# The feed-forward input projection of a two-layer trunk: seven half-size products replaced by eight plain ones with 512-column matmuls

## The chip, the cores and the metric

One core of a Trainium2 chip runs the whole program. The time is device microseconds of one execution. The kernel before took 2470.91 us, the median of 3 runs (2469.47 to 2471.38). The profiled execution is another one, of 2470.22 us, and its trace spans 2468.4 us of it; the other 1.8 us lie around the trace.

## The reference, cut to what matters

Two layers run over 512 tokens of width 1024. Each layer has a feed-forward block, a mixer of three attention kinds, a second feed-forward block and a gated per-layer input (called ple). Only the first product of a feed-forward block is changed:

```python
def swiglu(h, w_in, w_out):
    gate, up = jnp.split(h @ w_in, 2, axis=-1)
    return (jax.nn.silu(gate) * up) @ w_out

h = layer_norm(DEEPNORM_ALPHA * h + 0.5 * swiglu(h, ffa_w_in[i], ffa_w_out[i]), ln_g[i, 0], ln_b[i, 0])
```

`w_in` is 1024 x 5632 (gate and up, 2816 columns each) and `w_out` 2816 x 1024. There are four feed-forward blocks in a run: a and b in each of two layers.

## The kernel before, in words

**Three products for one.** Every projection is made in a reduced format, so each operand is held as a high part and a low remainder, and a product is the sum high x high, high x low, low x high: three matmuls into one PSUM bank (`mm3`, lines 401 to 405). The weights are split while the kernel runs. `Weights` (lines 48 to 116) loads a block of 128 x 1024 numbers with DMAs on SP's queue into one of 3 `wraw` tiles, ScalarE copies it to `whi` (line 72), and VectorE or GpSimd subtracts to get `wlo` (line 74). There are 4 pairs of `whi` and `wlo`, and `next()` prepares blocks up to 3 ahead of the one in use.

**Transposed activations.** `xT` holds the block's input, features on partitions, tokens along the free axis, as tiles `xh` and `xl`. `build_xT(t)` (lines 257 to 264) makes it for 128 tokens at a time: TensorE transposes `h[t]` into two banks of pool psA (`pa`, line 262), ScalarE copies the high part (line 254), VectorE subtracts the low (line 255). It is called for t = 0 to 3 at the end of the stage ahead, behind that stage's layer norm (lines 302 to 316) or ple update.

**The input projection before** (`ffn`, lines 420 to 535). The 2816 gate and 2816 up columns make 22 tiles of 128 + 128. Tiles 0 and 1 are plain (`part`): 8 slices of the inner dimension, three matmuls each, for gate and up, first over token columns 0 to 255 of both tiles, then over 256 to 511, so that work is there before the last tokens are. Their results lie in pools psB and psC (`pb`, `pc`). That is 2 x 2 x 2 x 8 x 3 = 192 matmuls of 256 columns.

The other 20 tiles use a Strassen-type scheme of one level (`product`, line 489). A tile's 1024 x 256 weights are cut in quarters, the 1024 x 512 activations too, and 7 products of sums and differences take the place of 8. Each product has 4 slices x 3 matmuls of 256 columns (lines 499 to 501), 84 matmuls a tile, into a gate bank of psI (`pi`) and an up bank of psA (`pa`). The price lies on the other engines. `add_sums` (lines 78 to 107) makes four sums of the weights per tile on VectorE (line 96, tiles `sa`, `sb`, `su`) and splits 7 quarters of 512 columns (lines 97 and 99). Lines 450 to 476 make sums of the activations, once per block. ScalarE takes partial results out of the banks (lines 503, 505, 507) and `close_tile` adds them up on VectorE around the Silu (lines 514 to 519).

**Behind it.** The output projection (lines 539 to 590) splits the result `g` (lines 546 and 547, tiles `gs` and `old`) and runs 512-column matmuls through `mm3` against blocks of `w_out`, 24 matmuls per block. It uses two halves of the output columns, `ps0` and `ps1`, four banks each. `ple_prepare` (lines 409 to 417), for block b only, takes two banks of psI in turn.

**What sets the order.** The order on each engine is fixed when the program is made. A planner with a model of the instructions' times places them by the order of the source and by what is ready; banks and buffers of one pool are handed out in the source's order. Each engine then runs its list strictly in turn.

Of the kernel before, what the change touches and what calls it, by code (L numbers as in the profile page):

```python
# [17 lines left out]
P = 128  # L18
S = 512
# [6 lines left out]
NC = 2  # L26
XA, XB, XV = 2, 2, ()
# [20 lines left out]
class Weights:  # L48
# [28 lines left out]

    def add_sums(self, fs, sums, first=False):

        nc = self.nc  # L80
        rest = ("s1", "s4", "s2", "a22", "s3")
        if first:
            todo = [(0, "a11"), (0, "a12"), (1, "a11"), (1, "a12")] + [(f, n) for f in range(2) for n in rest]
        else:
            todo = [(f, n) for f in range(2) for n in ("a22", "a11", "a12", "s1", "s2", "s4", "s3")]
        quarters = [None, None]

        def one(f, name, hi, lo):
            if quarters[f] is None:
                r0, r1 = self.load(fs[f][0], sums("raw")), self.load(fs[f][1], sums("raw"))  # L90
                quarters[f] = {"a11": r0[:, 0:512], "a21": r0[:, 512:1024], "a12": r1[:, 0:512], "a22": r1[:, 512:1024]}
            q = quarters[f]
            if "s1" not in q and (name == "s1" or not first):
                for s, x, y, op in (("s1", "a21", "a22", ALU.add), ("s3", "a11", "a21", ALU.subtract), ("s2", "s1", "a11", ALU.subtract), ("s4", "a12", "s2", ALU.subtract)):
                    q[s] = sums(s)
                    nc.vector.tensor_tensor(out=q[s], in0=q[x], in1=q[y], op=op)  # L96
            nc.scalar.copy(hi, q[name])  # L97
            e = nc.vector if name in ("s1", "s2", "s3") else nc.gpsimd
            e.tensor_tensor(out=lo, in0=q[name], in1=hi.bitcast(F32), op=ALU.subtract)  # L99

        for i in range(7):
            def make(i=i):
                hi, lo = self.pair()
                for j in range(2):
                    one(*todo[2 * i + j], hi[:, j * 512:(j + 1) * 512], lo[:, j * 512:(j + 1) * 512])
                return hi, lo
            self.blocks.append(make)
# [12 lines left out]
def trunk(  # L120
# [207 lines left out]
    def plan_ffn(l, w_in, w_out):  # L328
        def tile_in(f):
            return [[(lambda r, j=j: r.rearrange("p (j k c) -> p j k c", k=4, j=2)[:, j],  # L330
                      rows(w_in, l, kh * 4, 4, j * D_FF + f * P, j * D_FF + (f + 1) * P)) for j in range(2)] for kh in range(2)]

        def sums(name):
            if ln_s["new"]:
                ln_s["new"] = False
                ln_s["n"] = 0
                u = unit("su").rearrange("p a b -> p (a b)")
                ln_s["r"] = 0
                ur = unit("wr").rearrange("p a b -> p (a b)")
                ln_s["w"] = [None, None, None, ur[:, 0:1024], ur[:, 1024:]]  # L340
                ln_s["s"] = [lnp.tile([P, 1024], F32, tag="lng", name=nm("sa")), lnp.tile([P, 1024], F32, tag="lnb", name=nm("sb")), u[:, 0:1024], u[:, 1024:]]
            if name == "raw":
                ln_s["r"] += 1
                return ln_s["w"][(ln_s["r"] - 1) % 5]
            i = ln_s["n"] = ln_s["n"] + 1
            i = (i - 1) % 8
            return ln_s["s"][i // 2][:, (i % 2) * 512:(i % 2 + 1) * 512]

        for f in range(NC):
            for k, parts in enumerate(tile_in(f)):  # L350
                W.add(1024, parts, V if not W.blocks or (W.n == 0 and len(W.blocks) in XV) else None)
# [68 lines left out]
    def ffn(l, ln_i):  # L420
        ln_s["new"] = True
        GA = []

        def part(ps, us, c0, c1):
            for j in range(2):
                for k in range(KD):
                    hi, lo = (u.rearrange("p (j k c) -> p j k c", k=4, j=2)[:, j, k % 4, :] for u in us[k // 4])
                    mm3(ps[j][:, c0:c1], hi, lo, xT["hi"][:, k, c0:c1], xT["lo"][:, k, c0:c1], k == 0, k == KD - 1)

        def g_(f):  # L430
            if f % 4 == 0:
                GA.append(unit("g"))
            return GA[f // 4][:, f % 4, :]

        def evac(f, ps):
            s = slab("s")
            act(s, ps[0], AF.Silu)
            V.tensor_tensor(out=g_(f), in0=s, in1=ps[1], op=ALU.mult)

        us = [(W.next(), W.next()) for _ in range(2)]  # L440
        pss = [banks(), banks(True)]
        for f in range(2):
            part(pss[f], us[f], 0, 256)


        XH, XL = xT["hi"], xT["lo"]
        full = [unit("xf"), unit("xf")]

        B = {}
        for i, j in ((1, 1), (2, 1), (1, 2), (2, 2)):  # L450
            ks, cs = slice((i - 1) * 4, i * 4), slice((j - 1) * 256, j * 256)
            b = full[j - 1].rearrange("p a b -> p (a b)")[:, (i - 1) * 1024:i * 1024].rearrange("p (k c) -> p k c", k=4)
            (G if j == 1 else V).tensor_tensor(out=b, in0=XH[:, ks, cs].bitcast(F32), in1=XL[:, ks, cs].bitcast(F32), op=ALU.add)
            B[i, j] = b
        R = {"b11": (XH[:, 0:4, 0:256], XL[:, 0:4, 0:256]), "b21": (XH[:, 4:8, 0:256], XL[:, 4:8, 0:256]), "b22": (XH[:, 4:8, 256:512], XL[:, 4:8, 256:512])}
        todo = []
        for name, x, y in (("t1", B[1, 2], B[1, 1]), ("t3", B[2, 2], B[1, 2]), ("t2", B[2, 2], "t1"), ("t4", B[2, 1], "t2")):
            if name == "t3":
                hl = [XH[:, 0:4, 256:512], XL[:, 0:4, 256:512]]
            else:  # L460
                hl = unit(name, F32R).rearrange("p a b -> p (a b)").rearrange("p (w k c) -> p w k c", w=2, k=4)
                hl = [hl[:, 0], hl[:, 1]]
            d = {"t1": B[1, 1], "t3": B[1, 2], "t2": B[2, 2], "t4": B[2, 1]}[name]
            y = B[y] if isinstance(y, str) else y
            V.tensor_tensor(out=d, in0=x, in1=y, op=ALU.subtract)
            B[name] = d
            todo.append((name, hl, d))
# [6 lines left out]
        for x in todo:  # L474
            if x[0] != "t3":
                split_t(*x)
# [797 lines left out]
```

## Time and profile before

| What | Value |
| --- | --- |
| Median of 3 runs | 2470.91 us |
| Profiled execution | 2470.22 us |
| Its span in the trace | 2468.4 us |
| TensorE, share of the span busy | 93% |
| VectorE | 68% |
| GpSimd | 49% |
| ScalarE | 41% |
| DMA, main queue, share of 16 engines | 27.2% |
| Mean granted TensorE clock | 0.97 of 2.4 GHz |

PE is TensorE, DVE is VectorE, ACT is ScalarE, POOL is GpSimd. A matmul's duration in the trace runs from its start to the end of its last result, and the next starts before that; what a matmul costs in a stream is the distance from one start to the next. "Idle before" is the time in which the engine stood still, with what ended it. PEclk is the granted clock, 1.00 for 2.4 GHz and 0.50 for 1.2 GHz.

### The profile page before, as it was taken

The numbers are of one execution on the slowest core, as the hardware profiler recorded it, in microseconds if no ns is written. First come the engines' busy times: TensorE is split into PE (matmuls) and PEld (weight loads), VectorE is DVE, ScalarE is ACT, GpSimd is POOL, SyncE is SP. The second block draws the span as 40 slices with busy tenths as digits, with TensorE's granted clock in tenths as the row PEclk, the third lists the DMA queues.
The fourth block names the chain that finished last, engine by engine and source line by source line (L and its number), as shares of the span: only waits on it lengthen the run. The fifth ranks groups of instructions, "written<-read, shape, count | busy, mean of one in ns | idle before, by whom it ended". The sixth has DMA issues, their size and how long they took to land. (4 is left out here: it accounts for less than half of the span.)

```text
span 2468.4 us, 39369 instructions
## 1 busy us (share of the span) xinstructions
PE 2290.9 (93%) x15554; PEld 2000.7 (81%) x15554; DVE 1685.1 (68%) x2449; ACT 1022.8 (41%) x1929; POOL 1216.6 (49%) x785
## 2 busy tenths in 40 slices
PE   7999999998898899999989999999979997999998
PEld 7899888765777899988788998887657777999877
DVE  8899706559565899842589995075694668998334
ACT  4454513652452444532244544146424424445222
POOL 5555643434345655554365555424343466555542
PEclk9999999998999899999999999999999998999999
DMA  4333333211012233332323333332110122333322
GB/s 134 102 89 96 112 93 84 70 42 56 24 48 69 73 89 96 99 115 71 100 73 91 94 110 99 93 88 61 35 56 27 44 69 76 95 91 103 115 85 69
DMA packets 271272, 199.81 MB, mean 81 GB/s; under 512 B 12688, under 2 KB 236016, under 8 KB 271088
## 3 DMA queue, kind: packets, MB, share of 16 engines
q1 hardware_dynamic: 271088, 197.30, 27.2%
q8 instruction: 122, 2.00, 0.3%
q14 instruction: 62, 0.51, 0.1%
HBM read 195.17 MB, written 2.10 MB: 80 GB/s over the span
## 5 line engine op out<-in xcount | busy, mean ns | idle before, releaser
L74 POOL TENSOR_TENSOR wlo<-wraw,whi 128x1024 fp32r<-128x1024 f32 (+3 forms) x209 | 443.1, 2134 | 413.8 <-ACT whi L72 373.8
L72 ACT CAST whi<-wraw 128x1024 fp32r<-128x1024 f32 (+3 forms) x194 | 200.5, 1035 | 394.4 <-PE pi L405 156.7
L99 POOL TENSOR_TENSOR wlo<-wraw,whi 128x512 fp32r<-128x512 f32 x144 | 230.1, 1614 | 168.0 <-ACT whi L97 109.2
L499 PE MATMUL pa<-t,whi 128*128 128x256 f32 x640 | 191.3, 299 | 51.6 <-DVE g L518 27.9
L99 POOL TENSOR_TENSOR wlo<-wr,whi 128x512 fp32r<-128x512 f32 x96 | 153.9, 1616 | 132.7 <-ACT whi L97 127.9
L501 PE MATMUL pa<-t,wlo 128*128 128x256 f32 x640 | 177.8, 287 | 11.1 <-DVE wlo L99 11.1
L499 PE MATMUL pi<-xh,whi 128*128 128x256 f32 x640 | 185.5, 290 | 1.4 <-ACT whi L97 1.4
L501 PE MATMUL pa<-xh,wlo 128*128 128x256 f32 x640 | 182.1, 285 | 3.3 <-POOL wlo L99 3.3
L501 PE MATMUL pi<-xh,wlo 128*128 128x256 f32 x640 | 183.1, 286 | 0.0
L500 PE MATMUL pi<-xl,whi 128*128 128x256 f32 x640 | 183.0, 286 | 0.0
L500 PE MATMUL pa<-t,whi 128*128 128x256 f32 x640 | 182.9, 286 | 0.0
L499 PE MATMUL pa<-xh,whi 128*128 128x256 f32 x640 | 181.6, 284 | 0.0
L500 PE MATMUL pa<-xl,whi 128*128 128x256 f32 x640 | 181.6, 284 | 0.0
L499 PEld LDWEIGHTS pa<-t,whi 128*128 128x128 f32 x640 | 124.1, 194 | 67.2 <-DVE g L518 26.2
L187 ACT ACTIVATE s<-s 128x512 f32<-128x512 f32 x80 | 50.6, 632 | 258.2 <-DVE s L514 258.0
L97 ACT CAST whi<-su 128x512 fp32r<-128x512 f32 x160 | 91.7, 619 | 136.4 <-PE pi L500 118.9
L519 DVE TENSOR_TENSOR g<-g,s 128x512 f32<-128x512 f32 x80 | 140.2, 1752 | 1.1
L99 DVE TENSOR_TENSOR wlo<-su,whi 128x512 fp32r<-128x512 f32 x120 | 127.9, 1089 | 5.8 <-ACT whi L97 5.8
L501 PEld LDWEIGHTS pa<-t,wlo 128*128 128x128 f32 x640 | 121.9, 194 | 11.9 <-DVE wlo L99 11.9
L499 PEld LDWEIGHTS pi<-xh,whi 128*128 128x128 f32 x640 | 125.1, 195 | 3.8 <-ACT whi L97 1.9
L501 PEld LDWEIGHTS pa<-xh,wlo 128*128 128x128 f32 x640 | 123.5, 193 | 3.9 <-POOL wlo L99 3.9
L501 PEld LDWEIGHTS pi<-xh,wlo 128*128 128x128 f32 x640 | 124.9, 195 | 0.5 <-POOL wlo L99 0.4
(492 smaller groups left out, 7319.1 us busy)
## 6 DMA issues: line engine op xcount, KB each, us to landing
wraw<-in_ffa_w_in_dram SPq DMA_DIRECT2D x112, 256.0 KB, 3.8
wraw<-in_ffb_w_in_dram SPq DMA_DIRECT2D x112, 256.0 KB, 3.5
wraw<-in_ffa_w_out_dram SPq DMA_DIRECT2D x44, 512.0 KB, 3.8
wraw<-in_ffb_w_out_dram SPq DMA_DIRECT2D x44, 512.0 KB, 3.8
wraw<-in_mix_w_in_dram SPq DMA_DIRECT2D x40, 512.0 KB, 3.9
wr<-in_ffa_w_in_dram SPq DMA_DIRECT2D x64, 256.0 KB, 3.0
wr<-in_ffb_w_in_dram SPq DMA_DIRECT2D x64, 256.0 KB, 3.0
wraw<-in_mix_w_o_dram SPq DMA_DIRECT2D x16, 512.0 KB, 3.8
```

The lines of the kernel that those rows point to most:

```text
L72: self.nc.scalar.copy(hi[:, :width], raw[:, :width])
L74: (eng or self.nc.gpsimd).tensor_tensor(out=lo[:, c], in0=raw[:, c], in1=hi[:, c].bitcast(F32), op=ALU.subtract)
L97: nc.scalar.copy(hi, q[name])
L99: e.tensor_tensor(out=lo, in0=q[name], in1=hi.bitcast(F32), op=ALU.subtract)
L187: i = A.activation(*a, **k)
L499: T.matmul(dst, ah, bh, start=start and k == 0, stop=False, skip_group_check=True)
L500: T.matmul(dst, ah, bl, start=False, stop=False, skip_group_check=True)
L501: T.matmul(dst, al, bh, start=False, stop=k == 3, skip_group_check=True)
L519: V.tensor_tensor(out=g, in0=g, in1=s, op=ALU.mult)
```

## The change

All 22 tiles of the input projection are plain. They are taken two at a time: 11 steps, each with the gate of both tiles and then the up of both. A step has four weight blocks of 128 x 1024: (gate, inner slices 0 to 3), (gate, 4 to 7), (up, 0 to 3), (up, 4 to 7), each with 256 columns for the two tiles. A tile has 2 x 8 x 3 = 48 matmuls of 512 columns; in the first step alone the tokens are still taken in two halves of 256 columns, gate first in both halves, then up. Steps with an even number use two banks of psI (gate) and two of psA (up), the others psB and psC. Of a step's four low parts the first is subtracted on VectorE, the second and fourth on GpSimd, and the third on VectorE in every second step. `add_sums`, the sums of activations, `product` and `close_tile` are gone. `xh` and `xl` are two halves of one tile; `ps0` and `ps1` of the output projection take other banks.

```diff
-    def add_sums(self, fs, sums, first=False):
...
     def new_xT():
-        xT["hi"] = xp.tile([P, KD, S], F32R, tag="xh", name=nm("xh"))
-        xT["lo"] = xp.tile([P, KD, S], F32R, tag="xl", name=nm("xl"))
+        xT["x"] = xp.tile([P, 2, KD, S], F32R, tag="x", name=nm("x"))
+        xT["hi"], xT["lo"] = xT["x"][:, 0], xT["x"][:, 1]
...
     def plan_ffn(l, w_in, w_out):
...
-        for f in range(NC, NF, 2):
-            W.add_sums([tile_in(f), tile_in(f + 1)], sums, f == NC)
+        for f in range(0, NF, 2):
+            for i in range(2):
+                for j in range(2):
+                    W.add(1024, [(lambda r: r.rearrange("p (k c) -> p k c", k=4), rows(w_in, l, j * 4, 4, i * D_FF + f * P, i * D_FF + (f + 2) * P))],
+                          G if j or (i and f % 4) else V)
...
     def ffn(l, ln_i):
...
+        def part(ps, us, f, c0, c1):
+            for k in range(KD):
+                hi, lo = (u[:, (k % 4) * 256 + f * P:(k % 4) * 256 + (f + 1) * P] for u in us[k // 4])
+                mm3(ps[:, c0:c1], hi, lo, XH[:, k, c0:c1], XL[:, k, c0:c1], k == 0, k == KD - 1)
+
+        for i in range(NF // 2):
+            b = banks4() if i % 2 == 0 else banks() + banks(True)
+            sl = [slab("s"), slab("s")]
             for j in range(2):
+                us = (W.next(), W.next())
+                for c0, c1 in ((0, 256), (256, 512)) if i == 0 else ((0, 512),):
+                    for f in range(2):
+                        part(b[2 * j + f], us, f, c0, c1)
+                if j == 0:
+                    for f in range(2):
+                        act(sl[f], b[f], AF.Silu)
+                else:
+                    if i % 2 == 0:
+                        GA.append(unit("g"))
+                    for f in range(2):
+                        V.tensor_tensor(out=GA[i // 2][:, (i % 2) * 2 + f, :], in0=sl[f], in1=b[2 + f], op=ALU.mult)
...
-        ps0 = banks() + [ibank(), ibank()]
+        ps0 = banks() + banks(True)
...
-        ps1 = banks(True) + banks()
+        ps1 = [ibank(), ibank()] + banks()
```

## Rows read from the trace of the kernel before

**Rows 1.** The page's first line

```profile
span 2468.4 us, 39369 instructions
```

**Rows 2.** Windows: stretch, us, busy (x count) of PE, PEld, DVE, ACT, POOL; PEclk; DMA

```profile
41.40:283.40 242.00, 221.99 (x1722) 214.73 (x1721) 214.02 (x239) 116.24 (x232) 136.77 (x84) 0.98 0.32 91
...
814.20:1057.90 243.70, 222.00 (x1723) 215.17 (x1722) 217.42 (x242) 115.33 (x228) 139.72 (x85) 0.96 0.31 91
...
1269.40:1507.90 238.50, 220.61 (x1722) 212.76 (x1722) 211.93 (x237) 113.47 (x226) 135.61 (x84) 0.99 0.32 94
...
2041.00:2284.80 243.80, 220.79 (x1722) 214.07 (x1721) 217.45 (x241) 113.58 (x227) 140.25 (x84) 0.96 0.31 91
```

**Rows 3.** Lines by form: product matmuls (whole run), and output-projection ones in 41.4 to 283.4

```profile
L499 PE MATMUL pa<-t,whi 128*128 128x256 f32 x640 | 191.3, 299 | 51.6 <-DVE g L518 27.9 <-ACT s L503 21.5
...
L403 PE MATMUL pb<-whi,gs 128*128 128x512 f32 x10 | 3.6, 392 | 0.0
```

**Rows 4.** Timeline of PE: start, duration; six 256-column matmuls on, in the product stage

```profile
2205.71 0.28 PE L501 MATMUL pa<-t,wlo 128*128 128x256 f32 x1
...
2206.43 0.28 PE L501 MATMUL pa<-t,wlo 128*128 128x256 f32 x1
```

**Rows 5.** Waits of PE in the whole run: total us, times, longest us

```profile
PE pa L499 <- DVE g L518: 27.9, 37, 5.5
PE pa L499 <- ACT s L503: 21.5, 22, 2.0
```

**Rows 6.** Timeline of PE: six 512-column matmuls on, in the output projection

```profile
310.57 0.39 PE L403 MATMUL pi<-whi,old 128*128 128x512 f32 x1
...
311.93 0.39 PE L403 MATMUL pi<-whi,old 128*128 128x512 f32 x1
```

**Rows 7.** Timeline of PE: five 512-column matmuls on, in the mixer's projection

```profile
480.28 0.40 PE L403 MATMUL pi<-xh,whi 128*128 128x512 f32 x1
...
481.44 0.39 PE L405 MATMUL pi<-xh,wlo 128*128 128x512 f32 x1
```

**Rows 8.** Splitting and closing work: lines by form; then line source (min/median/max ns)

```profile
L72 ACT CAST whi<-wraw 128x1024 fp32r<-128x1024 f32 x180 | 188.7, 1050 | 381.3 <-PE pi L405 156.7 <-PE pb L405 123.5 <-PE pi L404 23.1
L74 POOL TENSOR_TENSOR wlo<-wraw,whi 128x1024 fp32r<-128x1024 f32 x139 | 353.7, 2552 | 318.1 <-ACT whi L72 285.2 <-issue 26.0 <-DVE gs L547 6.8
...
L74 DVE TENSOR_TENSOR wlo<-wraw,whi x33: 630/684/1226, 9.0 to 1688.2; 128x512 fp32r<-128x512 f32 x32, 128x1024 fp32r<-128x1024 f32 x1
...
L438 DVE TENSOR_TENSOR g<-s,pb x4: 672/674/689, 40.6 to 2041.5; 128x512 f32<-128x512 f32 x4
```

**Rows 9.** Windows: 60 us of the output projection

```profile
300.00:360.00 60.00, 60.00 (x267) 49.67 (x266) 5.36 (x8) 11.58 (x11) 28.36 (x12) 1.00 0.34 105
```

**Rows 10.** Windows: the four starts, from the first plain matmul to the first product

```profile
9.50:41.40 31.90, 29.31 (x209) 28.85 (x210) 30.38 (x37) 13.24 (x18) 19.61 (x9) 0.95 0.58 155
...
785.00:814.20 29.20, 27.78 (x212) 27.02 (x213) 22.41 (x26) 9.03 (x15) 19.20 (x10) 0.90 0.24 69
...
1240.30:1269.40 29.10, 26.52 (x208) 26.31 (x209) 28.23 (x21) 11.34 (x18) 19.50 (x8) 0.94 0.20 56
...
2009.00:2041.00 32.00, 28.64 (x212) 27.98 (x213) 28.15 (x26) 10.12 (x16) 20.29 (x11) 0.84 0.17 51
```

**Rows 11.** Timeline of PE: the last transposes of tokens at each start

```profile
22.58 0.96 PE L262 MATMUL pa<-ident,h 128*128 128x128 f32 x4 [1.89 <-DVE xl L255]
...
802.82 0.60 PE L262 MATMUL pa<-ident,h 128*128 128x128 f32 x4
...
1252.82 0.38 PE L262 MATMUL pa<-ident,h 128*128 128x128 f32 x2
...
2029.55 0.60 PE L262 MATMUL pa<-ident,h 128*128 128x128 f32 x4
```

**Rows 12.** One long wait in the product stage (timeline of PE), and the clock behind it (windows)

```profile
831.12 0.58 PE L501 MATMUL pa<-t,wlo 128*128 128x256 f32 x1 [5.06 <-DVE wlo L99]
...
831.00:836.00 5.00, 4.32 (x18) 4.03 (x19) 5.00 (x8) 1.78 (x4) 1.53 (x1) 0.50 0.18 52
```

More of the change, by code (lines that the diff above doesn't have):

```diff
@@ L76, in add @@
         self.blocks.append(make)
-    def add_sums(self, fs, sums, first=False):
[L80 to L107, printed above, removed]
     def fill(self, n):
@@ L328, in plan_ffn @@
     def plan_ffn(l, w_in, w_out):
[L329 to L351, printed above, removed]
-        for f in range(NC, NF, 2):
-            W.add_sums([tile_in(f), tile_in(f + 1)], sums, f == NC)
+        for f in range(0, NF, 2):
[3 more added lines that the diff above has]
+                          G if j or (i and f % 4) else V)
         for n in range(2):
@@ L435, in evac @@
[L435 to L467, printed above, removed]
@@ L469, in split_t @@
-        def split_t(name, hl, d):
-            A.copy(hl[0], d)
-            G.tensor_tensor(out=hl[1], in0=d, in1=hl[0].bitcast(F32), op=ALU.subtract)
-            R[name] = hl
-        for x in todo:
-            if x[0] != "t3":
-                split_t(*x)
-        for f in range(2):
-            part(pss[f], us[f], 256, 512)
-            evac(f, pss[f])
-        for f in range(2, NC):
-            u = (W.next(), W.next())
-            ps = banks(f % 2 == 1)
-            part(ps, u, 0, 512)
-            evac(f, ps)
@@ L485, in ffn @@
-        if NC > 2:
-            split_t(*todo[1])
-        blk = {"n": 0}
-        def product(ps, name, start):
-            up = name in ("t4", "b11", "t2", "t3")
-            dst = ps["up" if up else "gate"][:, 0:256] if name in ("t4", "b21") else ps["up" if up else "gate"][:, 256:512]
-            j = blk["n"] % 2
-            blk["n"] += 1
-            if j == 0:
-                blk["w"] = W.next()
-            hi, lo = (w_[:, j * 512:(j + 1) * 512] for w_ in blk["w"])
-            for k in range(4):
-                ah, al, bh, bl = hi[:, k * P:(k + 1) * P], lo[:, k * P:(k + 1) * P], R[name][0][:, k, :], R[name][1][:, k, :]
-                T.matmul(dst, ah, bh, start=start and k == 0, stop=False, skip_group_check=True)
-                T.matmul(dst, ah, bl, start=False, stop=False, skip_group_check=True)
-                T.matmul(dst, al, bh, start=False, stop=k == 3, skip_group_check=True)
-            if name == "b11":
-                A.copy(ps["s"][:, 0:256], dst)
-            elif name == "t1":
-                A.copy(ps["s5"], dst)
-            elif name == "t2":
-                A.copy(ps["s"][:, 256:512], dst)
@@ L509, in open_tile @@
-        def open_tile():
-            return {"gate": ibank(), "up": bank(), "s": slab("s"), "s5": slab("s5", 256)}
-        def close_tile(f, ps):
-            g, gate, up, s, s5 = g_(f), ps["gate"], ps["up"], ps["s"], ps["s5"]
-            V.tensor_tensor(out=s, in0=s, in1=gate, op=ALU.add)
-            act(s, s, AF.Silu)
-            V.tensor_tensor(out=g[:, 256:], in0=s5, in1=up[:, 256:], op=ALU.add)
-            V.tensor_copy(s5, up[:, 256:])
-            V.tensor_tensor(out=g[:, 0:256], in0=s5, in1=up[:, 0:256], op=ALU.add)
-            V.tensor_tensor(out=g, in0=g, in1=s, op=ALU.mult)
@@ L521, in ffn @@
[L521 to L535 removed]
+        XH, XL = xT["hi"], xT["lo"]
@@ L556, in split_unit @@
             if not spare:
-                old = [xp.tile([P, KD, S], F32R, tag=tag, name=nm("old")) for tag in ("xh", "xl")]
-                spare.extend(o[:, 4 * i:4 * i + 4, :] for o in old for i in range(2))
+                old = xp.tile([P, 2, KD, S], F32R, tag="x", name=nm("old"))
+                spare.extend(old[:, j, 4 * i:4 * i + 4, :] for j in range(2) for i in range(2))
             return spare[len(HL) - 5]
```

27 lines of the change are left out of this document (1 added, 26 removed).

## The prediction
> **What bounds the kernel now.** The page says that TensorE is busy for 93% of a span of 2468.4 us [rows 1], so I looked first at whether its busy time is full of work. The windows over the four product stages (20 tiles each, from the first product to the last) take 242.0, 243.7, 238.5 and 243.8 us, 968.0 together, at clocks of 0.96 to 0.99, and VectorE is busy for 212 to 217 us of each [rows 2]. The lines by form give the number of products: one group of 640 is 80 tiles x 2 products x 4 slices, so 7 products with three matmuls a slice are 6720 in all, 1680 a stage. The other 42 of the 1722 are taken as output-projection matmuls, 512 columns wide, that the planner drew forward [rows 2, 3].
>
> Then the timeline, for what a matmul costs. Six 256-column matmuls take 2206.43 - 2205.71 = 0.72 us, 0.120 each [rows 4]. Six 512-column ones take 311.93 - 310.57 = 1.36 us, 0.2267 each [rows 6]. So a stage holds 1680 x 0.120 = 201.6 us of products and 42 x 0.2267 = 9.5 of others, and the four hold 4 x 211.1 = 844.5 us. The remaining 123.5 us are waits, and slow clock behind waits. The waits view names their causes: an up bank that VectorE has not yet closed (27.9 us, L518), a bank that ScalarE has not yet emptied (21.5 us, L503) [rows 5]. One wait of 5.06 us for a weight remainder on VectorE is followed by a window at clock 0.50, 1.2 GHz [rows 12]. The reader should see two engines at their limit: TensorE has the work, and VectorE, nine tenths busy with making seven products out of eight, makes it stop about 1.5 us a tile (123.5 / 80).
>
> **The change part by part.**
>
> Matmuls. 80 tiles x 84 x 0.120 = 806.4 us go. 80 x 48 = 3840 matmuls of 512 columns come, at 0.2267: 870.5 us. That is 64.1 us **more**, all on TensorE and so on the path. The first two tiles of each block keep 192 matmuls of 256 columns. The 0.2267 is from the output projection; in the mixer's projection, which has the operands of the new code, five steps took 481.44 - 480.28 = 1.16 us, 0.232 each [rows 7]. I take 0.2267, since in that stretch VectorE is nearly idle [rows 9], which is nearer to the new stage than the crowded mixer. The other end is 3840 x 0.0053 = 20 us dearer; below 0.2267 nothing shows a gain.
>
> The Trainium skill, in TensorE: Matmul & The Clock Gate, section on the 56 ns gap, puts the distance of two matmuls at the columns over 2.4 GHz plus 2.5 ns. By this a product tile would cost 84 x 109.2 ns = 9.17 us and a plain one 48 x 215.8 ns = 10.36, 95 us more in 80 tiles and not 64, which speaks against the change. The trace doesn't agree: both widths stand 13.3 ns above their columns' time, and halving the number of matmuls saves that per matmul.
>
> Waits. With the sums, five partial drains and the closing additions gone, the 123.5 us lose their causes. Is something late next? A step of two tiles lasts 96 x 0.2267 = 21.8 us. In it ScalarE has four casts of 1.05 us and two Silus like the one that the old plain tiles had; GpSimd has two or three remainders of 2.55, at most 7.7 us; VectorE one or two of 1.23 to 2.55 (its single row of this width is the 1.226, GpSimd's is the upper bound) and two multiplications of 0.67, at most 6.4 us [rows 8]. Each is under a third of the step. A block serves 24 matmuls, 5.4 us, exactly as in the output projection, where one cast and one GpSimd remainder per block let TensorE run 60.00 of 60 us [rows 9]. The buffers hold two sets of two blocks. A set is 48 matmuls, 10.9 us; its first pair of buffers comes free after 36 of them, at 8.2 us, its second at the end; the refill takes 1.05 + 2.55 = 3.6 us and isn't wanted before 21.8. What queues behind a waiting cast on ScalarE is the Silu, whose bank is wanted two steps later. So the steady waits cost nothing; I leave 4 us (1 per block) for the first sets. Bounds: 0, and the third rival.
>
> The start of each block. Before, the first halves of two tiles were 96 matmuls, 11.5 us, that needed no late tokens. Now the up banks come from psA, which `build_xT` holds until the last transposes are emptied, so only the gate's 48 matmuls, 5.8 us, can run ahead, and 144 x 0.120 = 17.3 us must follow the last tokens. Those were transposed at 22.58, 802.82, 1252.82 and 2029.55 [rows 11]. Adding 2 us for transposing and emptying (an estimate; the four transposes alone show 0.4 to 1.0) and 17.3, the first pair would end at 41.9, 822.1, 1272.1 and 2048.9, against 41.4, 814.2, 1269.4 and 2041.0 now [rows 10]: 19.0 us later in sum if the tokens come no earlier. They should: their transposes stood in TensorE's list behind plain matmuls, and GpSimd and VectorE had the activation sums between the norm's steps. I take half of it off, and less for the fresh remainder on VectorE: +8 us. Bounds: the four starts last 122.2 us for 4 x 192 x 0.120 = 92.2 us of work, so at best 30 us less; at worst the 19, and the clock. The clocks of 0.84 to 0.95 mean that the worst start loses 32.0 x 0.16 = 5.1 us to it and all four 11.3 [rows 10]; all as bad as the worst would be 9 us more, +28.
>
> Smaller edits together. `ple_prepare` now waits for the first banks of `ps1`, since those are psI's: its eight transposes and four drains move into the tail of two blocks, beside the norm. I price it at 2 us, 0 to 8 (four drains of up to 1 us each, twice). The merged `x` tile, the loads of 256 instead of 128 columns (same bytes) and the free buffers of the sums cost nothing: DMA engines are a third busy in these windows [rows 2].
>
> Sum against the profiled execution: 2470.2 + 64.1 - 123.5 + 4 + 8 + 2 = 2424.8, about **2425 us**. The median of the runs is 0.7 us above the profiled execution, so it stands for both.
>
> **The rivals.**
>
> Late starts. The cover of 5.8 us is too short in every block, TensorE idles until the tokens are there, and it resumes at half clock. The +28 takes the place of the +8: 2445 us. For it: the clock of the start at 2009, 0.84 [rows 10], and the 0.50 behind a 5 us wait [rows 12]. Against it: the tokens' chain loses work. The Trainium skill, same page, section on why this matters, warns that a gap without matmuls puts the array back to half clock; rows 12 agree.
>
> Dearer wide matmuls. The new stage runs at the mixer's 0.232 [rows 7]: 20 us more, 2445. For it: same operands. Against: the mixer's engines are crowded.
>
> Late weights, **slower**. A set's two blocks are now released together instead of one by one. If the list of ScalarE or GpSimd lets the second block's conversion begin only as its set begins, its 3.6 us [rows 8] stand against 12 matmuls of the first block, 2.7 us, and each of 80 sets waits 0.9 us: 72 us more, 2497. It decides from 45 / 80 = 0.57 us a set. For it: before, the very same pair of engines held TensorE up at 1.5 us a tile. Against it: 10 us of slack per refill, and a third of the load.
>
> The page's fixed cost, with 95 for 64: 2456. The rows of both widths speak against it.
>
> **How the numbers follow.** Forecast 0.73, late starts 0.12, dearer matmuls 0.07, late weights 0.06, the page's cost 0.02. The forecast's own low end is starts that gain 8 us and no leftovers: 2403, say 2404. Upwards the late starts and dearer matmuls reach 2445, and with part of both 2452; what is left out above, late weights and both together, is about 0.1. A measurement of this kernel can tell about 0.2%, 5 us, from no change. Late starts and dearer matmuls together would end within it; I give that 0.04 out of their 0.19. Slower is the late weights, 0.06. Faster takes the rest, 0.90.
>
> **What would show it.** Right: from the second step on, matmuls 0.227 us apart without idle rows, some 217.6 us for 20 tiles; VectorE under a third busy there; no wait on L99, L503 or L518 and none in their place; clock 1.00. The starts show one gap between gate's first and second halves. Wrong: distances of 0.232 or more; idle of PE on `wlo` or `whi` at every set; a gap of over 5 us at each start with a clock of 0.5 after it; transposes of `ple_prepare` in front of the last norm.

## The result, and the profile after

The changed kernel took 2406.55 us, the median of 4 runs (2402.44 to 2414.78), against 2471.14 before on the same chip: a ratio of 0.9737, 95% interval 0.9705 to 0.9769. The forecast of 2425 lies 18 us above it, and 2406.55 lies in the range of 2404 to 2452, near its low end. The profiled execution is the longest of the four, 2414.78 us; stages are compared on its trace and, where it matters, on that of a second profiled execution of the same kernel (2406.48 us, run e1).

The page's first lines of the changed kernel:

```profile
span 2413.1 us, 30778 instructions
...
PE 2322.0 (96%) x12674; PEld 1903.3 (79%) x12674; DVE 910.9 (38%) x1612; ACT 799.3 (33%) x1273; POOL 860.0 (36%) x534
```

VectorE has fallen from 68% to 38% of the span, and TensorE has risen from 93% to 96%. The windows from the second step to the end of the eleventh (20 tiles) answer to [rows 2], with the same columns:

```profile
38.03:255.66 217.63, 217.63 (x962) 180.25 (x961) 35.38 (x38) 60.23 (x68) 63.60 (x27) 1.00 0.32 97
...
811.11:1028.70 217.59, 217.59 (x962) 180.25 (x961) 35.33 (x38) 58.73 (x66) 63.56 (x27) 1.00 0.32 99
...
1246.30:1464.00 217.70, 217.70 (x963) 180.32 (x962) 35.40 (x38) 60.24 (x69) 63.63 (x27) 1.00 0.31 97
...
2006.20:2223.80 217.60, 217.60 (x962) 180.19 (x961) 35.34 (x38) 58.73 (x66) 63.57 (x27) 1.00 0.32 99
```

TensorE's busy time equals the window in all four, at clock 1.00; ScalarE and GpSimd are busy for under 30% of it and VectorE for 16%. The timeline of PE in such a stretch, six matmuls apart:

```profile
899.77 0.39 PE L352 MATMUL pb<-x,whi 128*128 128x512 f32 x1
...
901.13 0.39 PE L352 MATMUL pb<-x,whi 128*128 128x512 f32 x1
```

901.13 - 899.77 = 1.36 us, 0.2267 each, as in [rows 6]. Among the waits of PE of the whole run, no wait of the input projection for weights or banks is left; its first matmuls wait 2.7 us in sum for tokens (L222). Of the four longest groups, L223 and L272 are the tokens and the norm, the other two stand in the mixer:

```profile
PE pa L230 <- DVE x L223: 18.5, 10, 4.0
PE pa L841 <- DVE K L842: 13.7, 4, 5.0
PE pi L351 <- DVE y L699: 11.7, 2, 5.8
PE pa L230 <- DVE ln_mv L272: 6.4, 2, 3.2
```

The four starts, answering to [rows 10], and then (timeline of PE) the last transposes of tokens, answering to [rows 11]:

```profile
9.78:38.03 28.25, 27.67 (x208) 27.38 (x209) 10.96 (x28) 13.05 (x17) 7.36 (x4) 1.00 0.54 180
...
781.08:811.11 30.03, 28.42 (x212) 27.83 (x213) 11.10 (x20) 9.72 (x13) 8.48 (x6) 0.89 0.38 124
...
1216.70:1246.30 29.60, 27.64 (x209) 27.34 (x209) 7.97 (x9) 7.17 (x10) 4.14 (x3) 0.87 0.22 67
...
1978.50:2006.20 27.70, 27.22 (x213) 26.77 (x213) 10.67 (x18) 9.76 (x13) 8.46 (x6) 0.93 0.40 128
```

```profile
20.57 0.60 PE L230 MATMUL pa<-ident,h 128*128 128x128 f32 x4
...
793.55 0.60 PE L230 MATMUL pa<-ident,h 128*128 128x128 f32 x4
...
1228.63 0.60 PE L230 MATMUL pa<-ident,h 128*128 128x128 f32 x4
...
1988.54 0.60 PE L230 MATMUL pa<-ident,h 128*128 128x128 f32 x4
```

The starts are shorter by some 6.5 us in sum. The last tokens come 10.8, 12.5, 11.9 and 10.0 us behind the first matmul, where they came 13.1, 17.8, 12.5 and 20.6 us behind it [rows 10, 11].

One stage grew. Windows over the two mixers, first of the kernel before, then of the changed one:

```profile
395.10:785.00 389.90, 358.00 (x2638) 279.15 (x2637) 251.91 (x544) 177.60 (x383) 159.13 (x146) 0.96 0.20 56
1619.50:2009.00 389.50, 359.59 (x2639) 281.04 (x2637) 246.62 (x545) 178.00 (x382) 157.29 (x146) 0.96 0.20 57
```

```profile
376.04:781.08 405.04, 372.15 (x2640) 290.62 (x2638) 254.91 (x545) 177.64 (x381) 154.77 (x144) 0.93 0.18 51
1584.40:1978.50 394.10, 360.47 (x2640) 280.67 (x2638) 252.87 (x547) 176.96 (x381) 154.02 (x144) 0.96 0.18 53
```

The first mixer has the same matmuls, 14 us more of busy time (372.15 against 358.00) and 33 us idle as against 32. The changed kernel's windows show where:

```profile
685.00:695.00 10.00, 8.99 (x53) 5.86 (x52) 4.31 (x11) 1.40 (x4) 1.26 (x2) 0.52 0.23 75
695.00:705.00 10.00, 10.00 (x81) 8.99 (x81) 5.09 (x19) 4.61 (x10) 5.31 (x4) 0.50 0.00 0
705.00:716.00 11.00, 11.00 (x68) 8.65 (x67) 3.80 (x11) 4.97 (x12) 3.66 (x3) 0.50 0.01 1
```

For 30.7 us, with TensorE busy nearly throughout, the granted clock is 0.50 (1.2 GHz); it falls at 685.4. In the kernel before the longest stretch at half clock is 13.7 us.

The whole, against the terms of the prediction, in us of the two profiled executions:

| Stage | Predicted | Measured |
| --- | --- | --- |
| Way to the first matmul | 0 | +0.2 |
| Four starts | +8 | -6.5 |
| From the second step to the end of the output projection, four times | +64.1 - 123.5 + 4 = -55.4 | -62.6 |
| Two mixers | 0 | +19.4 |
| ple and the tail | +2 | -5.8 |
| Sum | -45.4 | -55.3 |

### The profile page after: what moved, and what is told of

The parts are those of the page before. It is cut to its first block, busy times and chain, and to the rows that moved or that the text cites. A ratio compares the mean times of both kernels' runs of the same rounds, so it can differ in the third digit from the quotient of the medians.

```text
span 2413.1 us, 30778 instructions
## 1 busy us (share of the span) xinstructions
PE 2322.0 (96%) x12674; PEld 1903.3 (79%) x12674; DVE 910.9 (38%) x1612; ACT 799.3 (33%) x1273; POOL 860.0 (36%) x534
## 4 chain that ended last, share of the span: by engine, by line
PE 86%; DVE 10%; issue 2%; ACT 1%; POOL 1%; DMA 0%; SPq 0%; POOLq 0%; ACTq 0%; DVEq 0%
PE pi L351 9%; PE pi L352 9%; PE pi L353 9%; PE pb L352 7%; PE pb L353 7%; PE pb L351 7%; PE pc L351 5%; PE pc L353 5%; PE pc L352 5%; PE pa L353 4%; PE pa L351 4%; PE pa L352 4%; DVE X L797 1%; PE pb L925 1%; PE pa L743 1%
## 5 line engine op out<-in xcount | busy, mean ns | idle before, releaser
L73 POOL TENSOR_TENSOR wlo<-wraw,whi 128x1024 fp32r<-128x1024 f32 (+3 forms) x302 | 657.9, 2188 | 1121.9 <-ACT whi L71 1098.6
L71 ACT CAST whi<-wraw 128x1024 fp32r<-128x1024 f32 (+2 forms) x354 | 369.1, 1044 | 897.1 <-PE pc L353 172.8
L351 PE MATMUL pi<-x,whi 128*128 128x512 f32 (+1 forms) x704 | 266.7, 382 | 4.1 <-ACT x L222 2.7
L352 PE MATMUL pi<-x,whi 128*128 128x512 f32 (+1 forms) x704 | 268.0, 382 | 0.0
L353 PE MATMUL pi<-x,wlo 128*128 128x512 f32 (+1 forms) x704 | 266.7, 380 | 0.0
L353 PE MATMUL pa<-x,wlo 128*128 128x512 f32 (+1 forms) x448 | 160.7, 359 | 0.0
L351 PE MATMUL pa<-x,whi 128*128 128x512 f32 (+1 forms) x448 | 160.7, 359 | 0.0
L352 PE MATMUL pa<-x,whi 128*128 128x512 f32 (+1 forms) x448 | 160.7, 359 | 0.0
L351 PEld LDWEIGHTS pi<-x,whi 128*128 128x128 f32 x704 | 136.4, 195 | 30.7 <-issue 5.4
L353 PEld LDWEIGHTS pi<-x,wlo 128*128 128x128 f32 x704 | 137.1, 195 | 23.8 <-issue 1.0
L352 PEld LDWEIGHTS pi<-x,whi 128*128 128x128 f32 x704 | 136.8, 195 | 23.8 <-issue 2.1
L351 PE MATMUL pb<-x,whi 128*128 128x512 f32 x320 | 124.5, 389 | 0.0
L352 PE MATMUL pb<-x,whi 128*128 128x512 f32 x320 | 124.5, 389 | 0.0
L351 PE MATMUL pc<-x,whi 128*128 128x512 f32 x320 | 124.5, 389 | 0.0
L352 PE MATMUL pc<-x,whi 128*128 128x512 f32 x320 | 124.5, 389 | 0.0
L352 PEld LDWEIGHTS pa<-x,whi 128*128 128x128 f32 x448 | 84.7, 189 | 12.6
L351 PEld LDWEIGHTS pa<-x,whi 128*128 128x128 f32 x448 | 84.7, 189 | 12.4
```

The lines of the kernel that those rows point to most:

```text
L71: self.nc.scalar.copy(hi[:, :width], raw[:, :width])
L73: (eng or self.nc.gpsimd).tensor_tensor(out=lo[:, c], in0=raw[:, c], in1=hi[:, c].bitcast(F32), op=ALU.subtract)
L351: T.matmul(ps, ah, bh, start=first, stop=False)
L352: T.matmul(ps, ah, bl, start=False, stop=False)
L353: T.matmul(ps, al, bh, start=False, stop=last)
```

## The experiments

Times are medians; ratios are to the kernel before on the same chip. "Mixers" are the two stretches from an output projection's last matmul to the next input projection's first.

**e1, the changed kernel again.** No edit.

> The changed kernel once more, for a second profile. Its first profile lost some 15 us in the first mixer, where the same 477 matmuls ran with a clock of 0.50 for 30.7 us. Theory (that loss is the clock's and belongs to no edit): the four product stages are 217.6 us again, without a wait; the first mixer takes some 390 us and not 405, and the execution 2400 to 2410. Rival (the planner's new order costs the mixer its 15 us): the first mixer takes 405 again.

Measured: 2409.15 us, ratio 0.9738 (0.9701 to 0.9775). The projections are 217.6 us again and the starts 27.2, 30.0, 29.7 and 27.7. The first mixer is 400.3 us, not some 390: the 30.7 us at 0.50 are there again, at the same place. They belong to the kernel and not to that one execution, nearly as the rival had it.

**e2, the kernel before without the sums of the weights.** The quarters themselves stand in the place of the four sums that VectorE makes per tile.

```diff
-                for s, x, y, op in (("s1", "a21", "a22", ALU.add), ("s3", "a11", "a21", ALU.subtract), ...):
-                    q[s] = sums(s)
-                    nc.vector.tensor_tensor(out=q[s], in0=q[x], in1=q[y], op=op)
+                q["s1"], q["s2"], q["s3"], q["s4"] = q["a21"], q["a22"], q["a11"], q["a12"]
```

> The kernel before without VectorE's four sums of weights per tile: the products take raw quarters of the weights in their place, so the sums are left out of the result. Theory (VectorE's load makes TensorE wait in the product stages): VectorE's busy time there falls from some 215 to 120 us, the stages from 242 to between 208 and 220 us, and the whole by 90 to 130 us, to below the changed kernel's time. Rival (the waits come from the alternation of two banks and ScalarE's drains, whatever VectorE does): the stages stay above 230 us and the gain is under 45 us.

Measured: 2357.36 us, ratio 0.9526 (0.9480 to 0.9572), 116 us less, where the waits were put at 123.5. The first product stage, and the page's line:

```profile
41.30:278.00 236.70, 235.26 (x1827) 228.83 (x1826) 161.94 (x172) 127.20 (x239) 147.78 (x89) 1.00 0.35 104
```

```profile
PE 2249.1 (96%) x15554; PEld 1977.6 (84%) x15554; DVE 1402.7 (60%) x2129; ACT 1031.4 (44%) x1929; POOL 1196.0 (51%) x785
```

The stage now idles 1.4 us, the product matmuls untouched. The window holds 105 output matmuls more, 23.8 us; without them it would be 212.9 us, within the 208 to 220 expected. So the waits came with VectorE's four sums. Whether they came by the load on VectorE or by the place of each sum ahead of a split, this run does not separate. Seven products would be the faster way, if their sums, which this kernel leaves out of its result, cost nothing.

**e3, plain tiles before the others: 12 plain, 10 by seven products.** In the kernel before.

```diff
-NC = 2
+NC = 12
```

> The kernel before with 12 plain tiles ahead of 10 by products instead of 2 ahead of 20: half of the change, with no other edit. Theory (a plain tile costs 10.88 us and one by products 11.66 with its waits): 40 tiles x 0.78 = 31 us less, 2432 to 2446 us. Rival (only the removal of all sums frees VectorE, and the rest of the gain is in the starts and the output stage): under 15 us less.

Measured: 2428.36 us, ratio 0.9813 (0.9765 to 0.9861): 45 us less and not 31. From the first matmul to the end of the output projection the four blocks take 371.9, 371.1, 366.6 and 368.8 us; before they take 385.4, 385.7, 379.1 and 388.6, in the changed kernel 366.3, 369.0, 367.7 and 366.7. In sum that is 60 of the changed kernel's 69 us, with half of the tiles replaced. The ten product tiles of a block now hold 7.0 to 7.8 us beyond their matmuls, 0.7 a tile, where the twenty held 1.6 a tile; so the waits were not a fixed price per tile. Both mixers grew (393.4 and 407.0), with a stretch of 27.3 us and one of 30.7 us at half clock.

**e4 and e8, both kinds of tiles in turns.** If VectorE's load per us falls under its limit, the cheaper seven products could be had without their waits. e4 has 10 tiles by products and 12 plain; e8 has 8 and 14, and the sums of the activations behind the first tiles. The list of weights in e8's form, cut:

```diff
-        for f in range(NC, NF, 2):
-            W.add_sums([tile_in(f), tile_in(f + 1)], sums, f == NC)
...
+        for f in range(NC, NF - 2, 4):
+            at = len(W.blocks)
+            W.add_sums([tile_in(f), tile_in(f + 1)], sums)
+            late = W.blocks[at + 4:]
+            del W.blocks[at + 4:]
+            plain(f + 2)
+            W.blocks += late
+            plain(f + 3)
...
```

> Half of the tiles by products, half plain, in turns, so that VectorE's work for a product tile has two tiles' time: a product tile 10.08 us, a plain one 10.88. Theory (the fewer matmuls of the products are worth having once VectorE keeps up): the 20 tiles take some 210 us without waits against 217.6, 30 us less than the changed kernel in all, if the starts are like before's then 20 us less: 2378 to 2395 us. Rival (waits for banks and sums stay at 0.8 us or more per product tile): 2405 us or more, no better than the changed kernel.

> Tiles by products and plain ones in turns again, but 8 of 22 by products, the first of them after four plain tiles, the activations' sums made behind the first two tiles, and before's cover at the starts. Theory (the mixed kernel lost its gain in long waits for remainders at its first products, with the clock at half behind them): a block's input projection costs 23.0 + 10 x 10.88 + 8 x 10.08 us and next to no waits, 6 us a block less than the changed kernel, and shorter starts: 15 to 35 us less than it, 2372 to 2395. Rival (each product tile pays 0.8 us or more for its seven weights in turn, wherever it stands): no faster than the changed kernel within 8 us.

Measured: e4 2412.23 us, ratio 0.9754 (0.9720 to 0.9788); e8 2410.96, 0.9748 (0.9731 to 0.9766). Neither is under the changed kernel, as both rivals said. In e4 the first products wait for remainders of the weights (8.7, 6.2 and 4.4 us in three groups, up to 3.9 us at a time). The waits of PE of e8 show what took VectorE's place there, GpSimd, with 18.1 of the 29 us that TensorE stands idle in the four blocks:

```profile
PE pa L507 <- POOL wlo L99: 9.9, 4, 3.0
PE pa L506 <- POOL t L483: 8.2, 3, 2.9
```

From first matmul to the end of the output projection e8's four blocks take 1478.8 us, e1's 1468.6. The mixers of e8 take 393.3 and 389.9 us; their longest stretch at half clock is 17.1 us.

**e5 and e9, more work ahead of the last tokens.** The first halves of gate and up both run ahead, 96 matmuls, as before the change. Both give the first step the banks of psB and psC; e5 moves the banks of the output projection along, e9 keeps the pools that let `ple_prepare` stay late.

```diff
+            if i == 0:
+                first = [(W.next(), W.next()) for _ in range(2)]
+                for f in range(4):
+                    part(b[f], first[f // 2], f % 2, 0, 256)
...
```

Then e5, and below it e9:

```diff
-        ps0 = banks() + banks(True)
+        ps0 = banks4()
...
-        ps1 = [ibank(), ibank()] + banks()
+        ps1 = banks() + banks(True)
```

```diff
-        ps0 = banks() + banks(True)
+        ps0 = [bank(), bank()] + banks(True)
```

> The changed kernel with the cover given back: the first step takes banks of psB and psC, and the first halves of gate and up of both tiles (96 matmuls) run ahead of the second halves. Theory (at each start TensorE idles only while the last tokens are missing; the four starts of the changed kernel last 28.3, 30.0, 29.6 and 27.7 us for 23.0 of matmuls and some 2 of transposes): 1 to 3 us less at each start, 4 to 12 in all, product stages unchanged at 217.6. Rival (the starts are held by the clock and by the norm's chain, which no cover shortens): the same within 3 us.

> The start rearranged once more, with the PSUM banks of the output projection as in the changed kernel, so that the side input is again prepared late. Theory (the start's gain in the earlier form of this edit was real, and it was given back by the banks alone, through the projection of the side input): the four starts stay at some 25.9, 28.7, 27.1 and 28.6 us (5 us less in sum than in the changed kernel), and the two closing stages return from some 70.3 to 66.6 us each; with the mixers as in the earlier form (788 us in sum) the whole is some 2401 us, ratio 0.971. Rival: the closing stages' 4 us belonged to the rearranged start and not to the banks; they stay at 70 us, and the whole stays at some 2408 us, ratio 0.974.

Measured: e5 2408.35 us, ratio 0.9741 (0.9720 to 0.9762); e9 2412.72, 0.9753 (0.9737 to 0.9769). e5's starts are 25.9, 28.7, 27.1 and 28.6 us, 4.2 less in sum than e1's, but ple and the tail grow from 66.6 and 66.3 to 70.5 and 70.2 (before the change: 69.5 and 70.7), and the wait of the kernel before on the side input's projection is back:

```profile
PE pi L351 <- DVE PJ L1076: 4.4, 2, 2.2
```

In e9 that wait is gone from the leading waits, and ple and tail are 67.9 and 68.9; but the starts (27.0, 28.7, 29.4 and 26.7) kept only 2.8 us of the gain, and the mixers grew to 403.5 and 404.4, against 400.4 and 387.8 in e5. (The profiled execution of e9 is the longest of its four, 2421.8 us.) The edit brings nothing to the whole. With the late `ple_prepare`, ple and the tail are 1 to 4 us a time shorter in these runs; e9's 2401 us failed by the mixers above all.

**e6, the activation sums put back.** The changed kernel makes the old sums of the activations at each start, and nothing reads them.

```diff
...
+                            (G if q < 2 else V).tensor_tensor(out=d, in0=XH[...], in1=XL[...], op=ALU.add)
+                        for x, y in ((2, 0), (3, 2), (3, 0), (1, 3)):
+                            V.tensor_tensor(out=B[x], in0=B[x], in1=B[y], op=ALU.subtract)
...
```

> The changed kernel with before's sums of the activations (four additions, two of them on GpSimd, and four subtractions) made again at each start, with no reader. Theory (these sums stood between the steps of the norm on GpSimd and VectorE and held the tokens up; without them the last transposes at the second start came 12.5 us after the first matmul, with them 17.8): the last transposes come 3 to 5 us later at the two starts behind a mixer, and as the cover is 5.8 us, the starts lengthen by as much; 5 to 15 us in all. Rival (the tokens come earlier because the planner moved TensorE's transposes forward): under 3 us in all.

Measured: 2426.8 us, ratio 0.9811 (0.9772 to 0.9851). The two starts behind the mixers and their last transposes:

```profile
777.78:813.10 35.32, 30.97 (x213) 29.89 (x214) 20.84 (x26) 9.42 (x13) 13.57 (x8) 0.81 0.34 111
...
1978.91:2011.74 32.83, 29.62 (x215) 28.41 (x216) 20.95 (x26) 9.65 (x13) 13.57 (x8) 0.90 0.34 112
```

```profile
798.03 0.60 PE L230 MATMUL pa<-ident,h 128*128 128x128 f32 x4
...
1996.23 0.60 PE L230 MATMUL pa<-ident,h 128*128 128x128 f32 x4
```

They are 5.3 and 5.1 us longer than in the changed kernel, and the tokens come 20.2 and 17.3 us behind the first matmul, where they came 12.5 and 10.0 behind it. The other two starts changed by 0.9 and 0.1 us. The timeline of e6 shows the place on GpSimd, ahead of the norm's inverse square root (L240):

```profile
784.68 5.16 POOL L392 TENSOR_TENSOR xf<-x 128x1024 f32<-128x1024 f32 x2
...
789.81 0.54 POOL L240 TENSOR_TENSOR ln_r<-ln_w,mhalf 128x1 f32<-128x1 f32 x1
```

It comes 12.0 us behind the first matmul; in the changed kernel, without the two additions of 2.6 us each ahead of it, 6.0 us behind it. So the sums, queued between the norm's steps, held the tokens up behind the mixers. By how much was underestimated: 3 to 5 us were expected of the tokens and at most 15 of the whole, and the median of its two runs, 12.6 us apart, is some 18 us over e1.

**e7, all remainders on GpSimd.**

```diff
-                          G if j or (i and f % 4) else V)
+                          G)
```

> The changed kernel with all four remainders of a step on GpSimd. Theory (a third of the load and a whole set of slack): GpSimd's busy time rises from 63.6 to some 105 us of the 217.6 us stage, which doesn't get longer; the starts lose up to 2 us each as the first remainder stands in the norm's way; 0 to 8 us in all. Rival (late weights: the remainders follow each other and the second block of a set comes late): the stages grow by 0.5 us or more per set, 40 us or more in all.

Measured: 2430.39 us, ratio 0.9826 (0.9797 to 0.9855). The stages behind the starts stay at 217.6 us, so GpSimd alone would do there; the starts are 27.3, 31.8, 31.8 and 31.7, three of them 2 to 4 us longer. That is 8 us, as far as the theory went. The rest of the 21 us over e1 lies in the mixers, 402.8 and 406.3, with stretches of 37.5 and 30.7 us at half clock.

**e10, 256 columns in every step.** The changed kernel with twice the matmuls for the same work.

```diff
-                for c0, c1 in ((0, 256), (256, 512)) if i == 0 else ((0, 512),):
+                for c0, c1 in ((0, 256), (256, 512)):
```

> The changed kernel with 256-column matmuls in every step of the projection. Theory (a matmul of this form costs a fixed part beside its columns, by 0.120 us for 256 and 0.2267 us for 512 some 13.3 ns): 960 wide matmuls of each projection become 1920 narrow ones, 960 x 0.0133 = 12.8 us more in each, so 230.4 instead of 217.6 us from the second step to the last, and 51 us in all: some 2460 us, ratio 0.995. Rival (time goes by columns alone, and the narrow matmuls of the product tiles cost nothing of themselves): 217.6 us stays, and the whole is some 2408 us, ratio 0.974.

Measured: 2465.8 us, ratio 0.9967 (0.9956 to 0.9978). Window of the second stage:

```profile
826.30:1056.69 230.39, 230.39 (x1922) 230.39 (x1921) 32.37 (x36) 57.62 (x65) 62.30 (x27) 1.00 0.31 94
```

230.4 us as forecast, without idle. The doubled matmuls of the four stages cost 4 x 12.8 = 51 us, four fifths of what the change gains. (The whole is some 57 us over the changed kernel; most of the rest lies in the mixers, 409.4 and 391.3.) This is the price per matmul that the product tiles paid 84 times and the plain ones pay 48 times.

**e11, another order of the mixer.** The changed kernel, one step of the mixer's source put later in both layers.

```diff
- ... la00 mxa gz1 on2 go0 on3 ...
+ ... la00 mxa on2 gz1 go0 on3 ...
```

> The changed kernel with one entry of the mixer's order put one place later in both layers (the second half of the gate projection behind the third normalisation of the scan), so that the planner arranges the mixer otherwise; the projections are untouched. Theory (the 30 us at half clock in the first mixer come from where the planner puts the mixer's small matmuls and short waits, and not from the projection ahead of it): the stretch moves, shrinks or goes, and the first mixer moves away from 400 to 405 us, to some 390 us where it goes; product stages stay at 217.6 us. Rival (the projection ahead brings it, through the clock, whatever the mixer's order): the stretch stays at some 30 us, 305 to 310 us into the mixer, and the mixer at 400 to 405 us.

Measured: 2397.26 us, ratio 0.9693 (0.9671 to 0.9714), lower than the changed kernel by some 10 us, though the two intervals overlap at the edge. The theory failed where it was tested: the stretch neither moves, shrinks nor goes, but stays 305 us into the first mixer, as in e1, and is 37.5 us long. The first mixer takes 396.7 us, 4 less than in e1 and not some 390, the second 386.5, each with less idle time. The timeline of all engines around the place where the clock falls (start, duration; in brackets the wait ahead):

```profile
673.87 0.17 DVE L253 SCALAR_TENSOR_TENSOR of<-o_a,of 128x8 f32<-128x8 f32 x1
...
674.14 2.52 POOL L73 TENSOR_TENSOR wlo<-wraw,whi 128x512 fp32r<-128x512 f32 x2 [3.52 <-ACT whi L71]
...
674.54 0.92 DVE L251 TENSOR_TENSOR o_a<-of 128x8 f32<-128x8 f32 x1
...
675.38 1.36 DVE L678 TENSOR_SCALAR MW<-MW,su 128x128 f32<-128x128 f32 x1
...
676.89 0.30 PE L680 MATMUL pc<-ident,MW 128*128 128x128 f32 x1 [1.15 <-DVE o_a L252]
677.17 2.49 POOL L73 TENSOR_TENSOR wlo<-wraw,whi 128x512 fp32r<-128x512 f32 x2 [0.51 <-ACT whi L71]
...
678.49 1.19 DVE L251 TENSOR_TENSOR o_a<-of 128x8 f32<-128x8 f32 x1
...
680.35 0.69 PE L687 MATMUL pc<-MW,SVM 128*64 128x128 f32 x2 [1.03 <-DVE MW L682]
```

A VectorE operation over 8 columns lasts 0.17 us, but 0.92 and 1.19 beside a GpSimd remainder, and it ends where one of the remainders ends (674.54 + 0.92 = 675.46, with the first of two of 1.26 from 674.14; 678.49 + 1.19 = 679.68, with 677.17 + 2.49 = 679.66). The Trainium skill, SBUF — State Buffer, section on the two separate sides, says that the two engines share one pair of ports as an exclusive lock, so that the loser blocks for the whole instruction; these rows agree. Behind the held operation queues the softmax's scaling (L678), which itself lasts 1.36 us beside the second remainder, against 0.29 in e12 below. TensorE, which reads its result, waits 1.15 us; the row names the neighbour L252. From 679.6, within the second wait, the clock is 0.50. The traces of all kernels up to here hold 13 stretches of 27 to 38 us at half clock, all in mixers, and ahead of each stand the lengthened operations and the wait of 1.15 us. The second wait is not what brings the fall: in e10 the clock falls at 700.1, between the first wait and the second, which ends at 702.1 and is of 0.34 us. Before, e2 and e8 have no such stretch: in that part of the first mixer none of these operations is lengthened, and from 670 us on TensorE goes 30 us or more without a wait of over 0.3 us. The second mixers of before and e8 have two waits of 1.19 and 1.16 us, and half clock follows there too, but for 6.8 and 17.1 us. What sets the length is not shown.

**e12, those remainders on VectorE.** e11 with one engine changed in the first layer's mixer, for its first four output weights.

```diff
- ... "w_o0": "G" ...
+ ... "w_o0": "V" ...
```

> The kernel with the later gate projection, and in the first layer the remainders of the mixer's first four output weights on VectorE instead of GpSimd. Theory (in every run with the stretch at half clock, VectorE operations of 0.17 us in the scan's normalisation last 0.92 and 1.19 us, up to the end of a GpSimd remainder of 1.27 us beside them; what is queued behind them on VectorE makes TensorE wait for 1.15 and 1.02 us, and the granted clock falls to 0.50 for 30.7 to 37.5 us from the second wait on; the runs without the stretch have neither of the two waits): with no GpSimd remainder there the operations last 0.17 us again, the two waits go or fall under 0.5 us, and with them the stretch; at the changed kernel's price (14.8 us for 30.7 us) the 37.5 us give back some 18 us, of which VectorE's added work takes up to 3: the first mixer 396.7 -> some 380 us, the whole some 2381 us, ratio 0.962. Rival (the fall of the clock comes from the run of small matmuls itself, which no projection is put between): the stretch stays near 30 us, the first mixer at 395 us or more, the whole at some 2397 us, ratio 0.969.

Measured: 2393.55 us over 5 runs (2383.12 to 2395.75), ratio 0.9686 (0.9663 to 0.9709). Windows at the place, first of e11, then of e12:

```profile
680.00:690.00 10.00, 9.65 (x63) 6.66 (x64) 3.82 (x11) 1.43 (x5) 0.61 (x1) 0.50 0.17 54
690.00:700.00 10.00, 10.00 (x71) 8.73 (x68) 5.04 (x19) 5.43 (x11) 5.34 (x4) 0.50 0.01 2
700.00:710.00 10.00, 10.00 (x63) 7.90 (x63) 4.58 (x22) 4.28 (x10) 3.75 (x3) 0.50 0.00 0
```

```profile
680.00:690.00 10.00, 9.43 (x135) 7.18 (x134) 6.96 (x22) 5.29 (x17) 1.94 (x3) 1.00 0.17 60
690.00:700.00 10.00, 9.16 (x114) 7.57 (x110) 9.79 (x37) 9.51 (x22) 8.24 (x7) 1.00 0.03 5
700.00:710.00 10.00, 6.83 (x31) 5.17 (x30) 8.24 (x15) 3.74 (x10) 8.75 (x7) 0.60 0.14 50
```

The chain of holds, waits and half clock went as the theory said, and the price did not come. The operations last 0.15 to 0.17 us, both waits are gone, and twice as many matmuls run in the first 10 us, at full clock. But the first mixer takes 397.2 us as in e11: its busy time fell from 369.9 to 360.9 us and its idle time rose from 26.8 to 36.3. The waits of PE in 690 to 720 show part of it:

```profile
PE pb L945 <- DVE vn L928: 1.9, 1, 1.9
PE pi L353 <- POOL MXl L982: 1.3, 1, 1.3
PE pb L925 <- DVE state L940: 0.8, 1, 0.8
```

The longest of them, at 702.4, again stands behind a VectorE operation that is lengthened beside one of GpSimd (timelines of GpSimd and VectorE, e12):

```profile
699.75 1.58 POOL L975 TENSOR_TENSOR GZ<-GZ,V 128x512 f32<-128x512 f32 x1 [0.62 <-DVE V L959]
...
700.12 1.75 DVE L532 TENSOR_TENSOR GZ<-GZ,e 128x512 f32<-128x512 f32 x1
```

The same operation at this size (L532) lasts 0.67 us at the least. TensorE, faster, now waits for the scan's chain on VectorE, and 10.2 and 13.7 us at half clock follow later. So the slow stretch was, it seems, partly cover for a chain that would have made TensorE wait anyway. The moved remainders are not what fills VectorE there: it has 1.6 us of them between 680 and 690 and none from 690 to 710. e11 and e12 are the fastest that keep the whole computation; their intervals overlap with each other and, at the edge, with that of the changed kernel.

## Why the prediction was right, and where it was off

**In the range partly by luck.** The two large terms were right. But the rest of the sum was 32 us too high in e1's trace (7 in the projections, 16 in the starts, 9 in ple and the tail), and the mixers, for which the sum had no term, added 15. Without those the result would have been some 2392 us, below the low end of the range. That end is 2405 by the two terms it names (2424.8 - 16 - 4); 2403 needs ple's 2 us gone as well.

**Matmuls, +64.1: right.** 3840 at 0.2267 came out as 870.5 us over the four windows (217.63 + 217.59 + 217.70 + 217.60). The choice of the output projection's distance over the mixer's [rows 6, 7] held: no sign of 0.232. e10 measures the price per matmul directly and speaks against the 2.5 ns weighed in the prediction: 960 matmuls more in a stage cost 12.8 us, 13.3 ns each.

**Waits, -123.5: right.** e2 removes VectorE's sums alone and gains 116. What e3 adds is that they were not 1.5 us in every tile. Of the 42 matmuls of each window that the prediction took as output-projection ones, 40 are that by their tiles in the trace; this makes the waits 125.3.

**Leftovers, +4: nothing.** All four windows are without idle, so late weights, the slower rival, is out; e7 shows that even GpSimd alone keeps up there. With the matmuls as predicted and waits of 125.3 the stage should then have shrunk by 61.2 us; the other 1.4 us of the measured 62.6 were not followed up.

**Starts, +8: wrong in sign, -6.5.** The step that failed is "I take half of it off": the tokens come earlier by 2.3, 5.3, 0.6 and 10.5 us, by 18.7 in sum and not by half of 19.0. That alone would make the term +0.3. The rest is the 2 us set for transposing and emptying: the matmuls go on 0.4 to 0.5 us behind the start of the last four transposes, and the step ends 17.5 to 17.7 us behind it, not 19.3, four times. The prediction named the right cause, the sums between the norm's steps; e6 gives it its size, 7.7 and 7.3 us of the tokens behind the mixers. The short cover of 48 matmuls, on which late starts rested, costs 3 to 4 us in sum (e5, e9); that rival is out, for the longest wait in the four starts is 2.0 us.

**`ple_prepare`, +2: wrong in sign, -5.8 with the tail.** Later is better, since TensorE no longer waits for the side input's projection in ple (5.1 us before); e5, which puts the early banks back, puts back the wait and 4 us a time. How far it goes varies: the other kernels with the late form take 64.9 to 69.0 us.

**Mixers, 0: the step that was missing.** The code of the mixer is the same, but the order is made for the whole program, and the change gave it another: +19.4 us in the profiled execution, +14.8 in e1 (400.3 + 394.1 against 779.7). In the first mixer what grew is the time of the same matmuls, at half clock: busy time +14 and idle +1 in the profiled execution, +9 and +1 in e1. What stands ahead of the fall of the clock is shown by e11's rows and, by taking it away, by e12. That the stretch is the reason of the longer mixer is not shown: without it, in e12, the mixer is as long, and in e3 the first mixer takes 393.4 us with a stretch, as long as in e2 and e8 (393.4 and 393.3) without one. In e1's trace the starts (114.6 - 122.2 - 8 = -16) and ple and the tail (132.9 - 140.2 - 2 = -9) are errors of one kind, tokens and banks that come free earlier or later than thought.

What stays open: why the first mixer is still some 7 us above that of the kernel before when the stretch is gone, while the second, 381.7 us in e12, is 8 below, and which places in the list do it. With the source of the mixer unchanged, the two together take 779.7 us before and 783.2 to 809.1 in the other kernels; with e11's and e12's edits 783.2 and 778.9.

## What to carry to other kernels

Fewer multiplications are a gain only while the engine that makes the sums is not the bound; count the busy share of the helper in the stage itself, and price a matmul by its distance in a stream, with its fixed part, so that fewer and wider ones are credited for it. Where one planner orders the whole program, an edit in one stage moves others: compare the traces stage by stage, and treat a stage with the same code and a new time as a finding. A stall that is removed is worth only what the next wait leaves of it: e12 took away two waits and 37.5 us at half clock, and the mixer was as long as before.

## What the runs showed of the hardware that was not expected

A VectorE operation of 0.17 us on 8 columns is held to 0.92 and 1.19 us beside a GpSimd subtraction, and ends with it (e11). A wait of TensorE of 1.15 us, with matmuls of 64 and 128 columns behind it, stood ahead of each of 13 stretches of 27 to 38 us at 0.50; that of the changed kernel, 30.7 us, lasted while TensorE was busy for 9 to 10 of every 10 us. And the fixed part of a matmul of this form is 13.3 ns whether it is read from two streams of one kernel [rows 4, 6] or from one stage run at both widths (230.4 and 217.6 us).
